# One transformer layer on one core: the first MLP product in another visiting order, its stores on ScalarE's queue, its operands in tiles of their own

## The chip, the core and the metric

The kernel runs on one core of a Trainium2 chip. A core has TensorE (matmuls, PE in the profile), VectorE (DVE), ScalarE (ACT), GpSimd (POOL) and SyncE (SP, which only issues transfers); each runs its own instructions in order, and they meet by semaphores. Transfers between the chip's memory (DRAM) and the on-chip memory are issued from an engine's queue and carried by 16 DMA engines. The metric is the device time of one execution in microseconds (us).

## The reference

One layer of a diffusion backbone for 512 latent and 256 context tokens of width 2048, all in float32. Three groups of heads mix the tokens; their outputs are joined and projected; a squared-ReLU MLP of hidden width 8192 follows; both are gated and added to the stream.

```python
sh1, sc1, g1, sh2, sc2, g2 = _ada(c, ada_w[l], ada_b[l])      # silu(c) @ ada_w + ada_b, in six parts
hl = _modulate(_rmsnorm(x, norm1_w[l]), sh1, sc1)
y_c, y_l = _token_mixers(hc, hl, w_in[l], w_out[l], ...)      # y_l = concat(heads) @ w_out
x = x + g1 * y_l
x = x + g2 * _sq_relu_mlp(_modulate(_rmsnorm(x, norm2_w[l]), sh2, sc2), mlp_w1[l], mlp_w2[l])
return _rmsnorm(x, final_norm_w)

def _sq_relu_mlp(h, w1, w2):
    a = jax.nn.relu(jnp.einsum('btd,df->btf', h, w1))
    return jnp.einsum('btf,fd->btd', a * a, w2)
```

## The kernel before

**Precision.** Every large product is made of three: an operand is split into a rounded part and the rest (`hi`, `lo`), and `mm3` issues hi x hi, lo x hi and hi x lo as three matmuls (L171, L172, L173) into the same bank. A weight is loaded as float32 (`raw`, 128 x 1024, 0.5 MB), cast to `whi` by ScalarE (L94) and subtracted into `wlo` by VectorE (L95).

**Stages.** To 1048 us: normalisation, input projection, token mixers. Then the *output product* (four column groups of eight weight units, bank `yp`); beside it the rest of the adaLN product runs on VectorE (L120, loads at L133), its `raw` tiles from the same ring of three as the weights'. Then the *MLP input*: 64 transposes by matmul, four for each of 16 column groups (L956, `pt<-dg,x`), modulation by ScalarE (L972), and the sums and splits of the operands `hh`, `hl`, `hbh`, `hbl`. Then the two MLP products.

**Seven products for eight.** Both MLP products work by halves of both operands in the manner of Strassen and Winograd: seven products N1 to N7 of sums of halves stand for eight. `combine` (L938 to L941) makes the sums of the activations; the sums of the weights are made on the fly: N5 adds b12 to the N1 tile (VectorE, L1020), N6 and N4 add b22 and b21 to it by a transfer that accumulates (issued by POOL, L1024 and L1032), N7 adds N3's tile to b12's (POOL, L1029).

**The first product** has 32 blocks q of 256 hidden columns. A *visit* is one N of one block: 8 x 3 matmuls of 256 columns. Results meet in three banks per block: X takes N1, N6, N7 and N4, one on top of the other; Y takes N5 and N3; Z takes N2. Between two visits to X an engine must read the sum so far: after N1 ScalarE copies it (L1066), after N6 VectorE subtracts it from a copy of Y (L1073), after N7 the same (L1075), after N4 ScalarE copies it (L1077). Only then may the next visit add to the bank. Then ReLU and square (L1080, L1081), `combine`, a split into `xh` and `xl` (L1085, L1086), and two stores of 0.9 MB into `acd` (L1088, SyncE's queue).

**The order around the change.** The Python list `visits(32)` is TensorE's order. A tile scheduler places the other engines' instructions by data and by priority (`pri`): weights run ahead as far as the rings of tiles allow (seven `raw`, five pairs of splits), and each queue is then followed in order. So SyncE issues loads (L1009) and `acd` stores (L1088) in one sequence, and a store whose data isn't there holds up the loads behind it.

**The second product** has 16 blocks of seven visits of 24 matmuls of 512 columns; it loads its activations back from `acd` (`ao`, 1 MB, L1144) and adds each bank to `y`. At the end the gate (L1110), the residual `xr` (loaded at L1196, added by POOL, L1106), squares (L1117), the multiply by the norm's weight (POOL, L1119) and the row scaling follow.

Of the kernel before, what the change touches and what calls it, by code (L numbers as in the profile page):

```python
# [17 lines left out]
P = 128  # L18
# [29 lines left out]
def trunk_kernel(ctx: ExitStack, tc: tile.TileContext, a: dict, out: bass.AP, dbg: dict):  # L48
# [60 lines left out]
    def ada_units(blocks, fin):  # L109
# [12 lines left out]

        done = None
        for blk in blocks:
            with pri(APRI):
                ac = adap.tile([P, 512], F32, tag="adac", name="adac", bufs=2)
                G.memset(ac, 0.0)
                G.dma_start(out=ac[0:1, :], in_=a["ada2b"][blk:blk + 1, :])
            for u in range(8):
                add()  # L130
                with pri(APRI):
                    raw = wp.tile([P, 1024], F32, tag="raw", name="raw", bufs=3)
# [69 lines left out]
    hh = hp.tile([P, NK, T], F32R, name="hh")  # L202
    hl = hp.tile([P, NK, T], F32R, name="hl")
# [672 lines left out]
    ada = ada_units(range(12, 16), row_store)  # L876
    for n in range(4):
# [3 lines left out]
        for u in range(8):  # L881
            hi, lo = wunit(a["wo"][n, u], 1024)
# [42 lines left out]

    ctxm = ExitStack()
# [4 lines left out]
    hah = hh.rearrange("p k t -> p (k t)").rearrange("p (o k t) -> p o k t", o=4, k=8)  # L931
    hal = hl.rearrange("p k t -> p (k t)").rearrange("p (o k t) -> p o k t", o=4, k=8)

    PLACE = {"N1": 4, "N2": 5, "N3": 1, "N4": 6, "N5": 0, "N6": 2, "N7": 3}

    def combine(x):
# [4 lines left out]
        V.scalar_tensor_tensor(x[:, 1], x[:, 2], -1.0, x[:, 5], op0=ALU.mult, op1=ALU.subtract)  # L941

    hc = ctxc.enter_context(tc.tile_pool(name="hc", bufs=1))
    dg = [hc.tile([P, P], F32, name=f"dg{m}") for m in range(4)]
# [5 lines left out]
    for m in range(4):  # L950
        nc.sync.dma_start(out=x2d[m], in_=x2[:, m])
# [6 lines left out]
    order = [k for p in range(8) for k in (p, p + 8)]  # L958
    for k in order[:2]:
        pts[k] = acc.tile([P, 4, P], F32, tag="acc", name="pt")  # L960
        flip(k, (0, 1, 2))
    for i, k in enumerate(order):
        if i < 2:
# [4 lines left out]
        pt = pts[k].rearrange("p (h m) t -> p h (m t)", h=2)  # L968
        p = k % 8
        if k < 8:  # L970
            hx = hc.tile([P, 8, 256], F32, tag="hx", name="hx", bufs=3)
        S.activation(hx[:, 4:8:3] if k < 8 else hx[:, 5:7], pt, AF.Identity, bias=mod[:, 0, k:k + 1], scale=mod[:, 1, k:k + 1])  # L972
        if k >= 8:
            combine(hx)
            S.copy(hbh[:, :, p], hx[:, 4:7])
            V.tensor_sub(hbl[:, :, p], hx[:, 4:7], hbh[:, :, p].bitcast(F32))  # L976
            S.copy(hah[:, :, p], hx[:, 0:4])
            V.tensor_sub(hal[:, :, p], hx[:, 0:4], hah[:, :, p].bitcast(F32))  # L978
    ctxc.close()
    ctxp.close()  # L980

    def h_op(o, k):
        return (hah[:, o, k], hal[:, o, k]) if o < 4 else (hbh[:, o - 4, k], hbl[:, o - 4, k])

    class Weights:


        def __init__(self, extra, n_raw, n_split, start=None):
            self.extra, self.n_raw, self.n_split = extra, n_raw, n_split
            self.raws = self.splits = 0  # L990

        def raw(self):
            i = self.raws % (3 + self.n_raw)
            self.raws += 1
            if i < 3:
                return wp.tile([P, 1024], F32, tag="raw", name="raw", bufs=3)
            return self.extra.tile([P, 1024], F32, tag="raw2", name="raw", bufs=self.n_raw)

        def split(self, raw):
            i = self.splits % (2 + self.n_split)  # L1000
            self.splits += 1
            if i < 2:
                return split(wp, raw, 1024, 2)
            into = [self.extra.tile([P, 1024], F32R, tag=t + "2", name=t, bufs=self.n_split) for t in ("whi", "wlo")]
            return split(None, raw, 1024, 2, into)

        def load(self, src):
            t = self.raw()
            nc.sync.dma_start(out=t, in_=src)  # L1009
            return t  # L1010

        def operand(self, name, src, held, by):

            b11, b12, b21, b22 = src
            with pri(WPRI):
                if name in ("N1", "N2", "N3"):
                    t = held[name] = self.load({"N1": b11, "N2": b21, "N3": b22}[name])
                elif name == "N5":
                    t, held["b12"] = held["N1"], self.load(b12)
                    V.tensor_add(t, t, held["b12"])  # L1020
                elif name == "N6":
# [3 lines left out]
                    else:  # L1025
                        by.tensor_add(t, t, held["N3"])
# [16 lines left out]


    ctx1 = ExitStack()
    p1 = ctx1.enter_context(tc.tile_pool(name="p1", bufs=1, side="right"))
    wts = Weights(p1, 4, 3)
    held, bank, made, ac = {}, {}, {}, {}
    for q, name in visits(32):
# [6 lines left out]
        if new:  # L1056
            bank[q, which] = acc.tile([P, 512], F32, tag="acc", name="pa")
        b_ = bank[q, which][:, :256]
        for k in range(8):
            xh, xl = h_op(PLACE[name], k)  # L1060
            mm3(b_, wh[:, k], wl[:, k], xh, xl, new and k == 0, k == 7, skip=True)
        with pri(EPRI):
            if name in ("N1", "N5", "N3"):
                r = made[q, name] = p1.tile([P, 256], F32, tag="r", name="r", bufs=3)
# [13 lines left out]
        if name == "N4":  # L1078
# [8 lines left out]
            for i, y in enumerate((xh, xl)):  # L1087
                nc.sync.dma_start(out=acd[q // 4].rearrange("o p i b t -> p o i b t")[:, :, i, q % 4], in_=y.bitcast(F32))  # L1088
# [5 lines left out]
    p2 = ctx.enter_context(tc.tile_pool(name="p2", bufs=1, reuse_waits="tile"))  # L1094
    pr = ctx.enter_context(tc.tile_pool(name="pr", bufs=1, side="right", reuse_waits="tile"))
    wts = Weights(p2, 12, 3)
# [3 lines left out]
    def gate(m, n, last=None):  # L1100
# [12 lines left out]
    def squares(m, n, end=False):  # L1113
# [4 lines left out]
        if not end:  # L1118
            G.tensor_mul(y[:, m, cs], y[:, m, cs], fw[:, cs])  # L1119

    def finish_row(m, n):
# [5 lines left out]
        for c in rest:  # L1127
            c_ = slice(c * 512, (c + 1) * 512)
            if c == rest[-1]:
# [8 lines left out]
    for b, name in visits(nb):  # L1138
# [7 lines left out]
        w = [wts.operand(name, [a["w2"][g, j, h, i] for i in range(4)], held[b][h], V) for h in range(2)]  # L1146
        if b == 0 and name == "N1":
            y = p2.tile([P, 4, D], F32, name="y")
            gb2 = p2.tile([P, D], F32, name="gb2")
# [40 lines left out]
        if last:  # L1190
            if name == "N1":
                xr = {}
# [133 lines left out]
```

## Time and profile before

| | us |
|---|---|
| median of 3 runs (2672.55 to 2679.81) | 2678.2 |
| the profiled execution | 2679.46 |
| its span, first to last instruction | 2677.7 |
| TensorE busy | 2511.1 (94%) |
| VectorE busy | 1841.2 (69%) |
| ScalarE busy | 1156.0 (43%) |
| GpSimd busy | 435.5 (16%) |
| output product, MLP input, first and second MLP product begin at | 1048, 1242, 1270, 2010 |

The busy share is a mean over stages with different limits, so the stages are read apart: a table by stretch, then the waits of the engine that bounds it. In a row of a timeline the number in brackets is the idle time just before the instruction, and behind the arrow is what ended it. In a row of waits stand the engine and line that waited, what released it, and the total, the number and the longest of the waits. The clock is that granted to TensorE, as a share of full speed.

### The profile page before, as it was taken

The numbers are of one execution on the slowest core, as the hardware profiler recorded it, in microseconds if no ns is written. First come the engines' busy times: TensorE is split into PE (matmuls) and PEld (weight loads), VectorE is DVE, ScalarE is ACT, GpSimd is POOL, SyncE is SP. The second block draws the span as 40 slices with busy tenths as digits, with TensorE's granted clock in tenths as the row PEclk, the third lists the DMA queues.
The fourth block names the chain that finished last, engine by engine and source line by source line (L and its number), as shares of the span: only waits on it lengthen the run. The fifth ranks groups of instructions, "written<-read, shape, count | busy, mean of one in ns | idle before, by whom it ended". The sixth has DMA issues, their size and how long they took to land. (4 is left out here: it accounts for less than half of the span.)

```text
span 2677.7 us, 38869 instructions
## 1 busy us (share of the span) xinstructions
PE 2511.1 (94%) x15418; PEld 2274.0 (85%) x15418; DVE 1841.2 (69%) x2390; ACT 1156.0 (43%) x1595; POOL 435.5 (16%) x387
## 2 busy tenths in 40 slices
PE   8999999999999999998898989999887999999995
PEld 6879999998999988777898989999885888888874
DVE  8885666755444556555766767676666788988896
ACT  7664445522222234224555545555444433333333
POOL 0030000001001010001212222222212111111135
PEclk9999999999999999999899999999998999999998
DMA  9843333335454564655677878787769787777753
GB/s 327 296 165 111 109 117 111 128 109 175 131 166 144 158 185 149 222 191 178 185 222 216 232 214 226 214 235 215 209 199 343 243 249 249 219 238 229 230 169 119
DMA packets 182277, 524.03 MB, mean 196 GB/s; under 512 B 18864, under 2 KB 76464, under 8 KB 173264
## 3 DMA queue, kind: packets, MB, share of 16 engines
q1 hardware_dynamic: 157008, 444.78, 49.4%
q0 software_dynamic: 25088, 76.77, 13.8%
q8 instruction: 121, 1.98, 0.3%
q14 instruction: 60, 0.49, 0.1%
HBM read 446.47 MB, written 74.97 MB: 195 GB/s over the span
## 5 line engine op out<-in xcount | busy, mean ns | idle before, releaser
L94 ACT CAST whi<-raw 128x1024 fp32r<-128x1024 f32 (+1 forms) x644 | 661.1, 1038 | 942.1 <-PE yp L173 432.8
L95 DVE TENSOR_TENSOR wlo<-raw,whi 128x1024 fp32r<-128x1024 f32 (+1 forms) x644 | 863.1, 1347 | 282.9 <-ACT whi L94 281.6
L171 PE MATMUL yp<-whi,ao 128*128 128x512 f32 x896 | 350.8, 392 | 37.3 <-DVE gt L1110 18.7
L120 DVE SCALAR_TENSOR_TENSOR adac<-raw,csil,adac 128x512 f32<-128x512 f32 x256 | 192.0, 750 | 260.4 <-DMA raw<-in_ada_dram 251.5
L172 PE MATMUL yp<-wlo,ao 128*128 128x512 f32 x896 | 350.7, 391 | 4.6 <-DVE wlo L95 4.6
L171 PE MATMUL pa<-hh,whi 128*128 128x256 f32 x1024 | 300.3, 293 | 58.3 <-DVE ac L1073 52.3
L173 PE MATMUL yp<-whi,ao 128*128 128x512 f32 x896 | 349.9, 391 | 0.0
L172 PE MATMUL pa<-hl,whi 128*128 128x256 f32 x1024 | 297.5, 291 | 2.4 <-DVE hl L978 2.4
L173 PE MATMUL pa<-hh,wlo 128*128 128x256 f32 x1024 | 297.2, 290 | 0.0
L171 PEld LDWEIGHTS pa<-hh,whi 128*128 128x128 f32 x1024 | 204.1, 199 | 64.3 <-ACT r L1066 32.5
L171 PEld LDWEIGHTS yp<-whi,ao 128*128 128x128 f32 x896 | 169.0, 189 | 74.5 <-DVE gt L1110 19.1
L1029 POOL TENSOR_TENSOR raw<-raw 128x1024 f32<-128x1024 f32 x64 | 173.3, 2708 | 312.2 <-DMA raw<-in_w_dram 136.2
L171 PE MATMUL pa<-hbh,whi 128*128 128x256 f32 x768 | 218.8, 285 | 3.0 <-ACT hx L972 1.6
L172 PE MATMUL pa<-hbl,whi 128*128 128x256 f32 x768 | 218.7, 285 | 1.5 <-DVE hbl L976 1.5
L173 PE MATMUL pa<-hbh,wlo 128*128 128x256 f32 x768 | 218.6, 285 | 0.5 <-DVE wlo L95 0.5
L172 PEld LDWEIGHTS pa<-hl,whi 128*128 128x128 f32 x1024 | 204.0, 199 | 3.4 <-DVE hl L978 3.4
L173 PEld LDWEIGHTS pa<-hh,wlo 128*128 128x128 f32 x1024 | 203.6, 199 | 0.5
L172 PEld LDWEIGHTS yp<-wlo,ao 128*128 128x128 f32 x896 | 169.2, 189 | 41.0 <-DVE wlo L95 5.9
L173 PEld LDWEIGHTS yp<-whi,ao 128*128 128x128 f32 x896 | 169.3, 189 | 35.2
L171 PEld LDWEIGHTS pa<-hbh,whi 128*128 128x128 f32 x768 | 148.4, 193 | 3.9 <-ACT hx L972 1.8
L172 PEld LDWEIGHTS pa<-hbl,whi 128*128 128x128 f32 x768 | 148.6, 193 | 1.9 <-DVE hbl L976 1.9
L173 PEld LDWEIGHTS pa<-hbh,wlo 128*128 128x128 f32 x768 | 148.5, 193 | 0.7 <-DVE wlo L95 0.7
(382 smaller groups left out, 5253.6 us busy)
## 6 DMA issues: line engine op xcount, KB each, us to landing
raw<-in_w_dram SPq DMA_DIRECT2D x256, 512.0 KB, 6.0
raw<-in_ada_dram SPq DMA_DIRECT2D x192, 512.0 KB, 4.2
ao<-acd SPq DMA_DIRECT2D x56, 1024.0 KB, 7.4
raw<-in_w_dram POOLq DMA_DIRECT2D x96, 512.0 KB, 7.5
acd<-xh SPq DMA_DIRECT2D x32, 896.0 KB, 7.8
acd<-xl SPq DMA_DIRECT2D x32, 896.0 KB, 8.6
raw<-in_nb_dram SPq DMA_DIRECT2D x48, 512.0 KB, 3.6
raw<-in_wo_dram SPq DMA_DIRECT2D x32, 512.0 KB, 3.9
```

The lines of the kernel that those rows point to most:

```text
L94: S.copy(hi[:, :n], raw)
L95: V.tensor_sub(lo[:, :n], raw, hi[:, :n].bitcast(F32))
L120: V.scalar_tensor_tensor(ac, raw[:, kk * 512:(kk + 1) * 512], csil[:, 2 * u + kk:2 * u + kk + 1], ac, op0=ALU.mult, op1=ALU.add)
L171: TE.matmul(o, lh, rh, start=start, stop=False, skip_group_check=skip)
L172: TE.matmul(o, lh, rl, start=False, stop=False, skip_group_check=skip)
L173: TE.matmul(o, ll, rh, start=False, stop=stop, skip_group_check=skip)
L1029: G.tensor_add(t, t, held["N3"])
```

## The change

- **Output product.** The adaLN loads get a ring of three tiles of their own; of every four weight units two use further split tiles.
- **Operands.** `hh` and `hl` become four tiles each, and the three operands of `hbh`, `hbl` a pair of tiles each (`hb00` to `hb21`), so that a matmul waits for its own operand.
- **MLP input.** All 16 column groups are transposed and modulated in order; then the sums and the splits are made operand by operand, in halves, N1's first. The subtraction that POOL made in `combine` is VectorE's. The stores `x2d` are on ScalarE's queue.
- **First product.** `visits1` replaces `visits`. Z's bank comes from another pool. N1's loads have a ring of three, all others one of six; pairs of splits are four. N7's weight sum is VectorE's. The `acd` stores are on ScalarE's queue.
- **Second product.** Pools whose tiles are waited for one by one; `y` and `gb2` are made ahead; N7's weight sum stays on POOL, N6's on VectorE. In the last block `xr` is loaded at N5 into six weight tiles and one `ao` tile; POOL multiplies by the norm's weight for two of the four row groups only, VectorE does the others' in one instruction.

```diff
-    hbh = hb.tile([P, 3, 8, 256], F32R, name="hbh")
-    hbl = hb.tile([P, 3, 8, 256], F32R, name="hbl")
+    H += [[hb.tile([P, 8, 256], F32R, name=f"hb{o}{i}") for i in range(2)] for o in range(3)]
...
-        G.tensor_sub(x[:, 3], x[:, 4], x[:, 7])
+        V.tensor_sub(x[:, 3], x[:, 4], x[:, 7])
...
-        nc.sync.dma_start(out=x2d[m], in_=x2[:, m])
+        S.dma_start(out=x2d[m], in_=x2[:, m])
...
+    def h_split(o, x, q):
+        S.copy(H[o][0][:, q], x[:, q])
+        V.tensor_sub(H[o][1][:, q], x[:, q], H[o][0][:, q].bitcast(F32))
...
+        if k % 4 == 3:
+            q = qs_[k % 8 // 4]
+            if k < 8:
+                h_split(4, a11, q)
+                V.tensor_sub(a11[:, q], a11[:, q], a21[:, q])
+            else:
+                h_split(5, a12, q)
+                V.tensor_sub(a21[:, q], a22[:, q], a21[:, q])
...
                     t = held["b12"]
-                    G.tensor_add(t, t, held["N3"])
+                    (by or V).tensor_add(t, t, held["N3"])
...
+    def visits1(n):
+        out_ = [(0, "N1"), (0, "N2"), (1, "N1"), (1, "N2"), (0, "N5"), (1, "N5"), (0, "N3"), (0, "N6"), (1, "N3"),
+                (0, "N7"), (1, "N6"), (0, "N4")]
+        for b in range(2, n):
+            out_ += [(b, "N1"), (b, "N5"), (b - 1, "N7"), (b, "N2"), (b, "N3"), (b, "N6"), (b - 1, "N4")]
+        return out_ + [(n - 1, "N7"), (n - 1, "N4")]
...
-    wts = Weights(p1, 4, 3)
+    raw2, split2 = fresh(p1w, "raw2", 4), pair(p1w, "whi2", "wlo2", 2)
+    wts = Weights(lambda name: int(name != "N1"), [[wp_raw], [early] * 2 + [raw2] * 4],
+                  [wp_split] * 2 + [split2] * 2)
...
-                nc.sync.dma_start(out=acd[q // 4].rearrange("o p i b t -> p o i b t")[:, :, i, q % 4], in_=y.bitcast(F32))
+                S.dma_start(out=acd[q // 4].rearrange("o p i b t -> p o i b t")[:, :, i, q % 4], in_=y.bitcast(F32))
...
-            G.tensor_add(o, o, xr[m][:, cs])
+            G.tensor_add(o, o, xr[m, n // 2][:, 512 * (n % 2):512 * (n % 2 + 1)])
...
-        if not end:
+        if not end and m > 1:
             G.tensor_mul(y[:, m, cs], y[:, m, cs], fw[:, cs])
...
-                for m in {"N1": (0,), "N5": (1,), "N2": (2,), "N3": (3,)}.get(name, ()):
-                    xr[m] = pr.tile([P, D], F32, tag="ao", name="xr", bufs=8)
-                    nc.sync.dma_start(out=xr[m], in_=x2d[m])
+                elif name == "N5":
+                    for m in range(1, 4):
+                        for c in range(2):
+                            t = xr[m, c] = wts.raw(name)
+                            nc.sync.dma_start(out=t, in_=x2d[m][:, c * 1024:(c + 1) * 1024])
```

TensorE, in the middle of the first product, before: the first matmul of each of five visits. The number behind `pa` is the bank; `pa_13509` is block b's bank X, and the visits are N6(b), N1(b+1), N7(b), N5(b+1), N4(b).

```order
L171 MATMUL pa_13509<-hh_130,whi_13708 128x256
...
L171 MATMUL pa_13743<-hbh_11025,whi_13739 128x256
...
L171 MATMUL pa_13509<-hh_130,whi_13771 128x256
...
L171 MATMUL pa_13807<-hh_130,whi_13803 128x256
...
L171 MATMUL pa_13509<-hbh_11025,whi_13835 128x256
```

Now, from N6(b) on: bank X of block b is `pa_13719`, and the visits are N6(b), N4(b-1), N1(b+1), N5(b+1), N7(b).

```order
L171 MATMUL pa_13719<-hh2_132,whi_13876 128x256
...
L171 MATMUL pa_13485<-hb20_11035,whi_13906 128x256
...
L171 MATMUL pa_13953<-hb00_11031,whi_13949 128x256
...
L171 MATMUL pa_13987<-hh0_130,whi_13983 128x256
...
L171 MATMUL pa_13719<-hh3_133,whi_14015 128x256
```

The second visit to the same bank stood two visits after N6's and now stands four after it: one visit of another bank lay between, now three do.

ScalarE, one block of the first product from the relu on, before (`x2`, `x3`: so many in a row):

```order
L1068 ACTIVATE r<-pa 128x256
L94 CAST whi<-raw 128x1024
L1077 COPY ac<-pa 128x256
L1080 ACTIVATE ac<-ac 128x1024
L1081 ACTIVATE ac<-ac 128x1024
L94 CAST whi<-raw 128x1024
L1085 CAST xh<-ac 128x1792
L1068 ACTIVATE r<-pa 128x256
L94 CAST whi<-raw 128x1024 x2
```

And now, with the copy of bank X after N4 (L1133) and the two stores of the block:

```order
L1133 COPY ac<-pa 128x256
L1136 ACTIVATE ac<-ac 128x1024
L1137 ACTIVATE ac<-ac 128x1024
L1122 COPY r<-pa 128x256
L94 CAST whi<-raw 128x1024
L1141 CAST xh<-ac 128x1792
L1124 ACTIVATE r<-pa 128x256
L94 CAST whi<-raw 128x1024
L1144 DMA acd_106<-xh 128x7x256
L94 CAST whi<-raw 128x1024
L1144 DMA acd_106<-xl 128x7x256
L94 CAST whi<-raw 128x1024
```

Two store issues now stand among the casts of weights: that of `xh` behind its own cast and one of weights, that of `xl` one more cast of weights later.

SyncE, at the passage from the first to the second product, before (L1009 weight loads, L1088 `acd` stores, L1144 loads of the second product's operands):

```order
L1009 DMA raw<-in_w_dram 128x1024 x3
L1088 DMA acd_112<-xh 128x7x256
L1088 DMA acd_112<-xl 128x7x256
L1144 DMA ao<-acd_105 128x2048 x7
L1144 DMA ao<-acd_106 128x2048
L1088 DMA acd_112<-xh 128x7x256
L1088 DMA acd_112<-xl 128x7x256
L1009 DMA raw<-in_w_dram 128x1024 x18
```

And now (L1047 weight loads, L1209 operand loads):

```order
L1047 DMA raw<-in_w_dram 128x1024 x131
L1209 DMA ao<-acd_105 128x2048 x2
L1047 DMA raw<-in_w_dram 128x1024
L1209 DMA ao<-acd_105 128x2048
L1047 DMA raw<-in_w_dram 128x1024 x2
L1209 DMA ao<-acd_105 128x2048
L1047 DMA raw<-in_w_dram 128x1024 x2
L1209 DMA ao<-acd_105 128x2048
L1047 DMA raw<-in_w_dram 128x1024 x2
```

The last four stores and the operand loads stood ahead of the second product's weight loads; now no store is in this queue, and operand and weight loads alternate.

## Rows read from the trace of the kernel before

**Rows 1.** Busy time of each engine by stretch of the span.
```profile
core 0: us, PE busy (x) PEld busy (x) DVE busy (x) ACT busy (x) POOL busy (x), PEclk, DMA share, GB/s
1048.00:1242.00 194.00, 182.59 (x776) 146.95 (x775) 111.89 (x148) 57.42 (x85) 11.66 (x20) 0.98 0.61 203
1242.00:1270.00 28.00, 19.14 (x134) 17.92 (x134) 21.43 (x43) 19.78 (x33) 5.53 (x8) 0.88 0.51 174
1270.00:1303.00 33.00, 25.98 (x163) 23.33 (x162) 26.39 (x29) 19.38 (x25) 11.94 (x7) 0.79 0.42 129
1303.00:2009.00 706.00, 649.01 (x5215) 642.52 (x5214) 488.29 (x466) 367.08 (x433) 168.24 (x122) 0.97 0.77 219
2009.00:2050.00 41.00, 22.00 (x83) 16.85 (x84) 19.36 (x15) 13.30 (x16) 7.23 (x3) 0.75 1.02 404
2050.00:2606.00 556.00, 556.00 (x2454) 460.40 (x2453) 483.35 (x462) 223.36 (x218) 108.12 (x64) 1.00 0.74 230
2606.00:2678.00 72.00, 37.96 (x153) 29.67 (x151) 49.64 (x72) 26.81 (x57) 37.33 (x26) 0.81 0.35 117
```

**Rows 2.** Waits of TensorE in the first product, 1303 to 2009 us.
```profile
PE pa L171 <- DVE ac L1073: 52.3, 21, 5.9
```

**Rows 3.** Timeline of TensorE at one of these waits: start, us, instruction.
```profile
1406.61 0.28 PE L173 MATMUL pa<-hbh,wlo 128*128 128x256 f32 x1
...
1410.43 0.36 PE L171 MATMUL pa<-hh,whi 128*128 128x256 f32 x1 [3.54 <-DVE ac L1073]
```

**Rows 4.** Timeline of VectorE: output product, then the first product.
```profile
1173.34 0.75 DVE L120 SCALAR_TENSOR_TENSOR adac<-raw,csil,adac 128x512 f32<-128x512 f32 x1 [5.82 <-DMA raw<-in_ada_dram]
...
1406.79 2.02 DVE L1086 TENSOR_TENSOR xl<-ac,xh 128x1792 fp32r<-128x1792 f32 x1 [0.67 <-ACT xh L1085]
...
1409.87 0.41 DVE L1073 TENSOR_TENSOR ac<-r,pa 128x256 f32<-128x256 f32 x1
...
1449.60 3.18 DVE L95 TENSOR_TENSOR wlo<-raw,whi 128x1024 fp32r<-128x1024 f32 x1 [0.45 <-ACT whi L94]
```

**Rows 5.** Waits of TensorE in the output product, 1048 to 1242 us.
```profile
PE yp L172 <- DVE wlo L95: 10.3, 4, 3.6
```

**Rows 6.** Waits of TensorE between the products, 2009 to 2050 us.
```profile
PE yp L171 <- ACT whi L94: 17.2, 2, 15.6
```

**Rows 7.** Timeline of SyncE: one store's issue, and the second product's loads.
```profile
1406.79 0.38 SPq L1088 DMA_DIRECT2D acd<-xh  x1
...
2020.80 26.58 SPq L1009 DMA_DIRECT2D raw<-in_w_dram  x15
```

**Rows 8.** Waits of TensorE at the end, 2606 to 2680 us.
```profile
PE yp L171 <- DVE gt L1110: 18.7, 1, 18.7
PE yp L172 <- DVE wlo L95: 4.0, 2, 2.6
```

**Rows 9.** Groups by line, 1303 to 2009 us: count, busy, mean ns, idle before.
```profile
L95 DVE TENSOR_TENSOR wlo<-raw,whi 128x1024 fp32r<-128x1024 f32 x217 | 292.4, 1362 | 119.4 <-ACT whi L94 118.8
L1020 DVE TENSOR_TENSOR raw<-raw 128x1024 f32<-128x1024 f32 x31 | 38.0, 1225 | 9.8 <-DMA raw<-in_w_dram 9.0
L938 DVE TENSOR_TENSOR ac<-ac 128x256 f32<-128x256 f32 x31 | 30.1, 970 | 2.4 <-ACT ac L1081 2.3
```

**Rows 10.** Waits of SyncE in the first product, 1303 to 2009 us.
```profile
SPq L1088 <- ACT r L1068: 145.9, 31, 17.1
SPq L1088 <- DVE xl L1086: 57.8, 31, 3.9
```

**Rows 11.** Timeline of TensorE at the first product's first matmul.
```profile
1269.63 0.39 PE L171 MATMUL pa<-hbh,whi 128*128 128x256 f32 x1 [1.61 <-ACT hx L972]
```

**Rows 12.** Timeline of SyncE and of POOL at the end.
```profile
2623.54 5.76 SPq L1196 DMA_DIRECT2D xr<-x2d  x2
2628.62 8.84 POOL L1106 TENSOR_TENSOR y<-y,xr 128x512 f32<-128x512 f32 x5 [0.87 <-DMA xr<-x2d]
```

**Rows 13.** DMA issues of the first product: count, KB each, us to landing.
```profile
raw<-in_w_dram SPq DMA_DIRECT2D x120, 512.0 KB, 7.8
```

More of the change, by code (lines that the diff above doesn't have):

```diff
@@ L107, in trunk_kernel, with ada_units @@
     mod = adap.tile([P, 2, NK], F32, name="mod")
-    def ada_units(blocks, fin):
+    def ada_units(blocks, fin, ring=None):
         late = []
@@ L201, in trunk_kernel, with __init__, __getitem__ @@
     hp = ctxh_.enter_context(tc.tile_pool(name="hT", bufs=1, side="right"))
-    hh = hp.tile([P, NK, T], F32R, name="hh")
-    hl = hp.tile([P, NK, T], F32R, name="hl")
+    class Four:
+        def __init__(self, name):
+            self.tiles = [hp.tile([P, 4, T], F32R, name=f"{name}{i}") for i in range(4)]
+        def __getitem__(self, at):
+            return self.tiles[at[1] // 4][(at[0], at[1] % 4) + at[2:]]
+    hh, hl = Four("hh"), Four("hl")
     ams = hp.tile([P, NK, 4], F32, name="ams")
@@ L881, in trunk_kernel @@
         for u in range(8):
-            hi, lo = wunit(a["wo"][n, u], 1024)
+            into = None
+            if n_unit % 4 > 1:
+                into = [postb.tile([P, 1024], F32R, tag=t, name=t, bufs=2) for t in ("whi3", "wlo3")]
+            n_unit += 1
+            hi, lo = wunit(a["wo"][n, u], 1024, into=into)
             step(ada)
@@ L917, in row_rstd, with fresh, pair, new @@
         return y
+    def fresh(pool, tag, bufs):
+        first = [pool.tile([P, 1024], F32, tag=tag, name="raw", bufs=bufs)]
+        return lambda: first.pop() if first else pool.tile([P, 1024], F32, tag=tag, name="raw", bufs=bufs)
+    def pair(pool, hi, lo, bufs):
+        def new():
+            return [pool.tile([P, 1024], F32R, tag=t, name=n, bufs=bufs) for t, n in ((hi, "whi"), (lo, "wlo"))]
+        first = [new()]
+        return lambda: first.pop() if first else new()
     ctxm = ExitStack()
@@ L950, in trunk_kernel @@
     for m in range(4):
-        nc.sync.dma_start(out=x2d[m], in_=x2[:, m])
+        S.dma_start(out=x2d[m], in_=x2[:, m])
+    Av = [hc.tile([P, 2, 8, 256], F32, name=f"A{i}") for i in range(2)]
+    a11, a21, a12, a22 = Av[0][:, 0], Av[0][:, 1], Av[1][:, 0], Av[1][:, 1]
     pts = {}
@@ L956, in flip @@
             TE.matmul(pts[k][:, m], x2[:, m, k * P:(k + 1) * P], dg[m], start=True, stop=True)
-    order = [k for p in range(8) for k in (p, p + 8)]
-    for k in order[:2]:
+    def h_split(o, x, q):
+        S.copy(H[o][0][:, q], x[:, q])
+        V.tensor_sub(H[o][1][:, q], x[:, q], H[o][0][:, q].bitcast(F32))
+    for k in range(6):
         pts[k] = acc.tile([P, 4, P], F32, tag="acc", name="pt")
         flip(k, (0, 1, 2))
-    for i, k in enumerate(order):
-        if i < 2:
+    qs_ = (slice(0, 4), slice(4, 8))
+    for k in range(NK):
+        if k < 6:
             flip(k, (3,))
@@ L979, in trunk_kernel, with __init__, next, raw @@
+    for o, x in ((1, a12), (2, a21), (3, a11), (6, a22)):
+        for q in qs_:
+            h_split(o, x, q)
     ctxc.close()
     ctxp.close()
-    def h_op(o, k):
-        return (hah[:, o, k], hal[:, o, k]) if o < 4 else (hbh[:, o - 4, k], hbl[:, o - 4, k])
     class Weights:
[L988 to L997, printed above, removed]
-        def split(self, raw):
[L1000 to L1008, printed above, removed]
+        def __init__(self, ring_of, raws, splits):
+            self.ring_of, self.raws, self.splits = ring_of, raws, splits
+            self.used = {}
+        def next(self, ring, tiles):
+            i = self.used.get(ring, 0)
+            self.used[ring] = i + 1
+            return tiles[i % len(tiles)]()
+        def raw(self, name):
+            ring = self.ring_of(name)
+            return self.next(ring, self.raws[ring])
+        def split(self, raw):
+            return split(None, raw, 1024, 2, self.next("split", self.splits))
+        def load(self, name, src):
+            t = self.raw(name)
@@ L1145, in trunk_kernel @@
         t = aops[g, name]
[L1146 to L1149, printed above, removed]
+        w = [wts.operand(name, [a["w2"][g, j, h, i] for i in range(4)], held[b][h], G) for h in range(2)]
         new = name in ("N1", "N5", "N2")
```

78 lines of the change are left out of this document (47 added, 31 removed).

## The prediction

> **What bounds the kernel now.** I read the table by stage first [rows 1]: for each stretch its length, the busy time of each engine, the granted clock and the DMA share. The second MLP product (2050 to 2606 us) is TensorE without a gap: 556.00 us busy in 556.00, clock 1.00. The first MLP product (1303 to 2009) is not: 649.01 busy in 706.00, clock 0.97. So the time to be had lies in the first product and in the short stretches between stages, and the next view is what TensorE waits for in each.
>
> In the first product 52.3 us of the 57.0 idle go to one place: 21 waits of up to 5.9 us for the subtraction at L1073 [rows 2]. That subtraction takes the sum after visit N6 out of bank X before N7 may add to it. Between N6 and N7 of a block the old order has one other visit, N1 of the next block, 24 matmuls or 2.9 us at the 0.12 us that a matmul of 256 columns takes (706 us less idle and clock loss, below, over 5215). The timeline shows why 2.9 us don't do [rows 3, 4]: N1's last matmul starts at 1406.61; VectorE is then in L1086 (2.02 us from 1406.79), behind it a weight split, and L1073 starts only at 1409.87 and takes 0.41; TensorE goes on at 1410.43 after 3.54 us of waiting.
>
> The other stretches, in the same two views. Output product (1048 to 1242): 10.3 us in four waits for a weight split L95, clock 0.98 [rows 1, 5]; at one of them VectorE had stood 5.82 us for an adaLN weight load [rows 4], whose tiles come from the same ring of three as the product's own weights. MLP input (1242 to 1303): 61.00 us with 45.12 busy and clocks of 0.88 and 0.79. Between the products (2009 to 2050): 22.00 busy in 41.00, of which 17.2 are two waits for whi [rows 6]; SyncE issues the fifteen weight loads only from 2020.80 [rows 7], behind the last acd stores. The end (2606 to 2678): 37.96 busy in 72.00, with one wait of 18.7 us for gt at L1110 [rows 8].
>
> **The change part by part.** The sum is made against the profiled execution, 2679.46 us with a span of 2677.7; the median of the runs shown is 2678.2, 1.3 lower.
>
> *First product.* Loss now: 57.0 idle, and the clock: 0.03 of 706, some 21 (the mean is rounded: 18 to 25). The stretch without waits shows 1.00 and every stretch with waits less [rows 1], so I let the clock loss go with the waits. Together 78, 2.5 a block over 31 blocks. The new order puts three visits between N6 and N7 in bank X (N4, N1, N5: 8.6 us) and three between N7 and N4 (N2, N3, N6). L1073 needs 0.41 and what is queued ahead of it on VectorE, at most one L1086 and two L95: 0.4 + 2.0 + 2 x 1.4 = 5.2 [rows 4, 9]. So the wait goes. What is late next is VectorE's own load: 488.29 us in 31 blocks, 15.8 a block, plus the two additions that POOL did (L1029, L939), which at VectorE's price for such shapes (L1020 and L938, 1225 and 970 ns, [rows 9]) are 2.2: 18.0 of the 20.2 us that 168 matmuls take. Part of the 15.8 is lengthened: one L95 beside POOL's L1029 took 3.18 [rows 4], the mean is 1362 ns [rows 9]; without POOL's additions I expect 16. So it fits in the mean, with 2 to 4 us a block to spare, and I leave 8 us for places where it doesn't. Gain 70; bounds 40 (one us a block is lost) and 78 (nothing is).
>
> *The acd stores move to ScalarE's queue.* SyncE stood 145.9 us for xh and 57.8 for xl in this stage [rows 10], 6.6 a block, with weight loads queued behind. Now these waits stand in ScalarE's queue: xh's is the cast just ahead on that engine, and xl's costs at most what lies between its cast and VectorE's split. Behind the store are casts of weights, four pairs of split tiles deep. An issue takes 0.38 us on SyncE [rows 7]; ScalarE's own is not shown for this tile, so I take the same: 0.8 a block beside ScalarE's 367.08 / 31 = 11.8 [rows 1], and count nothing, hidden by 7.6 us of slack. If that cover is gone it is the slower rival below.
>
> The Trainium skill (DMA: Bandwidth & Descriptors, "Issuing engines are not separate DMA queues") speaks against this step: DMAs issued from the several engines share the same 16 DMA engines and interleave, and issuing from more of them saves only the sequencer's issue time. By that rule the move is worth 62 x 0.38, or 24 us of SyncE's time and none of TensorE's; the row on SyncE shows waits in order, 203.7 us, which the rule does not count. My sum gives the move no term of its own, so both readings give the same time.
>
> *Output product.* The adaLN loads get a ring of their own, two of four weight units other split tiles. Of 10.3 us of waits and some 4 of clock (0.02 of 194) I take 9; from 0 (VectorE still works in order through the adaLN sums) to 15.
>
> *MLP input.* The first product's first matmul now stands at 1269.63, behind a wait of 1.61 us for a scaling [rows 11]. Work per operand in halves lets N1 begin when its operand is there, while N3, N6 and N4 are split later; but all 16 scalings come before in order, three POOL subtractions become VectorE's, and b12's load waits for memory of the flips' tiles. VectorE is busy 47.82 of 61.00 us here [rows 1] and gets more. I take a gain of 4, a quarter of TensorE's 15.9 us of idle; from a loss of 13 (VectorE becomes the bound, and the 13 us in which it doesn't work come on top) to a gain of 10, two thirds of that idle.
>
> *Between the products.* SyncE's loads of the second product no longer stand behind the acd stores, and their tiles come free one by one. Of 19 us idle I take 11 back. What is late next is the DMA: the share is 1.02 at 404 GB/s already [rows 1], and the 15 loads of 0.5 MB with the operands of 1 MB need 19 us at that rate, of which some 8 come before the first pairs stand. From 0 to 20.
>
> *The end.* SyncE issued two of the four xr loads at 2623.54 [rows 12], and POOL's additions that need them ran 2628.62 on for 8.84 us; squares, and so gt, came after, and the wait of 18.7 followed. xr is now loaded at N5 of the last block, and fewer products lie on POOL. What is late next is the split of the last N4 weights, which waits for an accumulating load and stands ahead of the gate's product on VectorE. The stage loses 22.7 to waits [rows 8] and some 3 to the clock while busy; I keep 8 and 3 of these, so the gain is 15; from 0 to 25.
>
> Sum: -70 - 9 - 4 - 11 - 15 = -109, so 2679.5 - 109 = 2570, and with the 1.3 to the median 2569. I say 2570.
>
> **Rivals.** *VectorE is the bound* in the first product: with 18.0 of 20.2 in order, subtractions come late in the new place and 1.3 us a block are lost, 40 more: 2610. For it: L95 has the most busy time there [rows 9]. Against it: three visits of cover.
>
> *The DMA engines are.* The share was 0.77 over 706 us [rows 1]; the same bytes in 628 + 8 make 0.85. If loads (7.8 us from issue to landing now, [rows 13]) stretch, a block takes 21.5: also 2610. Against it: 0.74 in the second product at no loss.
>
> *The first product gains, the edges don't* (transition and end turn one wait into another): 2570 + 26 = 2596.
>
> *Slower: ScalarE stands before its stores.* If the 6.6 us a block of SyncE's waits all come to stand on ScalarE, the casts behind are 6.6 late each block; one visit (2.9) of finished pairs covers part, or none: 3.7 to 6.6 a block lost, 115 to 205 us, in the mean 160: 2570 + 160 = 2730. It decides from 3.5 us a block (109 / 31). Against it: most of the 145.9 is SyncE waiting for ScalarE's own earlier work, which in ScalarE's queue is no wait.
>
> *The change doesn't do what it says*: the pools let tiles free later than written, so that the loads come as late as before and the stall is only renamed: 2660 to 2690, about the same.
>
> **How the numbers follow.** What a measurement can tell from no change is about 0.3%, 8 us. Forecast (2545 to 2595) 0.46; VectorE 0.18; DMA 0.14; edges 0.10; slower by ScalarE 0.06; nothing done 0.06. Of the last I give half to no change, a third to slower. Faster is 0.46 + 0.18 + 0.14 + 0.10 = 0.88 and a little, 0.89; same 0.03; slower 0.08. The range reaches from 2535, where the edges give all and the first product all, to 2630, past the two cases at 2610 with their own spread; it leaves out the slower case, the undone one, and a few in a hundred below.
>
> **What would show it.** In the profile after: TensorE's waits in the first product without L1073's successor (the subtraction after N6), busy share above 0.97, clock 1.00; SyncE's waits for xh and xl gone and none of more than 2 us in ScalarE at its stores; no wait for gt over 8 us at the end; the first weight loads of the second product landing before its first matmul is due. I am wrong if TensorE waits 1 us a block or more for a split, or if ScalarE's idle time at the stores is 3 us a block.

## The result, and the profile after

| | us |
|---|---|
| changed, median of 4 runs (2600.21 to 2605.4) | 2602.68 |
| before, median of 4 runs beside them (2672.55 to 2679.81) | 2677.57 |
| ratio, 95% interval | 0.9723 [0.9706, 0.974] |
| profiled execution, its span | 2605.4, 2603.6 |

The forecast was 2570 with a range from 2535 to 2630. The time fell by 75 us where 109 were summed. The kernel after by stage, as in [rows 1] (columns: stretch, its length, busy us of PE, PEld, DVE, ACT, POOL with counts, clock, DMA share, GB/s):

```profile
1050.00:1244.00 194.00, 178.84 (x770) 145.22 (x769) 116.76 (x152) 55.58 (x85) 11.50 (x20) 0.96 0.61 210
1244.00:1264.00 20.00, 16.56 (x131) 15.88 (x130) 8.60 (x21) 13.38 (x25) 0.55 (x1) 0.91 0.71 262
1264.00:1300.00 36.00, 20.35 (x148) 19.24 (x146) 35.23 (x32) 23.02 (x28) 2.63 (x3) 0.84 0.58 161
1300.00:1935.00 635.00, 631.78 (x5227) 631.42 (x5228) 466.76 (x526) 373.24 (x434) 51.82 (x61) 0.99 0.85 238
1935.00:2000.00 65.00, 55.55 (x223) 43.06 (x222) 43.66 (x39) 31.01 (x36) 12.97 (x6) 0.92 0.91 325
2000.00:2040.00 40.00, 40.00 (x174) 32.41 (x173) 31.73 (x29) 18.03 (x20) 8.29 (x4) 1.00 1.02 370
2040.00:2540.00 500.00, 500.00 (x2163) 404.80 (x2162) 430.21 (x416) 189.55 (x181) 96.88 (x59) 1.00 0.74 225
2540.00:2604.00 64.00, 34.73 (x138) 26.21 (x136) 48.99 (x71) 21.57 (x51) 27.47 (x18) 0.83 0.27 82
```

The first product is full: 631.78 of 635 busy, where 57 were idle. The start of that product, the output product and the end have idle time and a low clock as before. The next table takes each stage's length from the start times of its matmuls. Where the row doesn't say "whole", the matmuls themselves are taken off, at the pace of the stretches without a gap: 0.12007 us for 256 columns (first product, after) and 0.22667 us for 512 (second product, before). The columns "before" and "after" are then what is left, the time lost:

| us lost | before | after | gain | forecast |
|---|---|---|---|---|
| output product, first to last matmul's start (whole) | 193.9 | 195.3 | -1.4 | 9 |
| from there to N1's first matmul (whole) | 27.8 | 20.5 | 7.3 | 4, with the next row |
| first product, matmuls 0 to 168 | 13.8 | 21.0 | -7.2 | |
| first product, 168 to 5200 | 70.5 | 0.0 | 70.5 | 70 |
| its last visits and the second product's first 336 matmuls | 31.8 | 21.2 | 10.6 | 11 |
| second product, 336 to 2500 | 0.0 | 10.1 | -10.1 | 0 |
| rest to the last instruction | 37.4 | 33.1 | 4.3 | 15 |
| sum | | | 74.0 | 109 |

What TensorE waits for after the change, in four stretches (line that waited, releaser, total, times, longest): the output product, the start of the first product, the passage, the end.

```profile
PE yp L171 <- ACT whi L94: 13.1, 1, 13.1
...
PE pa L171 <- ACT r L1122: 10.3, 1, 10.3
...
PE yp L171 <- ACT whi L94: 4.9, 1, 4.9
...
PE yp L171 <- DVE gt L1173: 12.7, 2, 12.0
PE yp L172 <- DVE wlo L95: 2.1, 3, 0.8
```

The 52.3 us of [rows 2] and the 17.2 of [rows 6] are gone or small, the 18.7 of [rows 8] is 12.0, and two waits are new. The places behind them, in the timelines after (start, us, engine, instruction, idle before and its releaser):

```profile
1071.62 1.99 ACT L94 CAST whi<-raw 128x1024 fp32r<-128x1024 f32 x2 [0.80 <-DVE hl L787]
...
1297.54 0.37 ACT L1122 COPY r<-pa 128x256 f32<-128x256 f32 x1 [4.97 <-DVE hl L991]
...
1950.79 1.69 ACT L1141 CAST xh<-ac 128x1792 fp32r<-128x1792 f32 x1 [7.18 <-DMA acd<-xh]
...
2560.57 0.63 ACT L1180 ACTIVATE sq<-y 128x512 f32<-128x512 f32 x1 [10.09 <-POOL y L1169]
...
2572.80 2.13 DVE L95 TENSOR_TENSOR wlo<-raw,whi 128x1024 fp32r<-128x1024 f32 x1 [2.54 <-ACT whi L94]
2574.85 0.68 DVE L1173 TENSOR_TENSOR gt<-yp,gb 128x512 f32<-128x512 f32 x1
```

In the output product the cast into the further split tiles starts only when the token mixers' last split (L787) is done: the new pool lies on memory of their tiles, and adaLN loads wait there too. At the start of the first product the copy of N1's bank (L1122) starts only when VectorE has made the last operand splits (L991): the built program puts the copy's tile at 92704, inside the MLP input's tile A0 (92128 to 108512), and so it must wait until A0 has been read. At the passage ScalarE's cast of xh waits 7.18 us for the store of the block before, and the next weight cast stands behind it. At the end the gate's product stands on VectorE behind the split of N4's last weights, whose cast stood on ScalarE behind squares that waited for POOL.

The loss from 336 to 2500 is of another kind: no wait, clock 1.00, and still 2163 matmuls in 500 us where the kernel before made 2207:

```profile
2050.00:2550.00 500.00, 500.00 (x2207) 414.04 (x2206) 429.86 (x411) 202.25 (x198) 91.28 (x55) 1.00 0.77 237
```

By their start times, in the mean of each tile, the matmuls that stream from the two old pairs of split tiles are followed by the next in 227 to 232 ns, those from the three new pairs in 233.2 to 233.4; before, all in 226.7. The built program puts the new pairs at 131040 and on, 96 modulo 128 bytes; before they lay at 75552 and on, 32 modulo 128, as do the old pairs in both kernels.

### The profile page after: what moved, and what is told of

Its sections match the earlier page's. It is cut to its first block, busy times and chain, and to the rows that moved or that the text cites. A ratio compares the mean times of both kernels' runs of the same rounds, so it can differ in the third digit from the quotient of the medians.

```text
span 2603.6 us, 38694 instructions
## 1 busy us (share of the span) xinstructions
PE 2499.1 (96%) x15418; PEld 2257.0 (87%) x15418; DVE 1821.4 (70%) x2440; ACT 1156.6 (44%) x1589; POOL 298.4 (11%) x309
## 4 chain that ended last, share of the span: by engine, by line
PE 44%; DVE 4%; DMA 2%; ACT 1%; issue 1%; POOL 0%; ACTq 0%; SPq 0%; DVEq 0%; POOLq 0%
PE pa L172 8%; PE pa L171 8%; PE pa L173 8%; PE yp L172 7%; PE yp L171 7%; PE yp L173 7%; DVE wlo L95 2%; DMA acd<-xl 2%; DMA raw<-in_w_dram 1%; DVE y L1168 0%; DVE y L1248 0%; ACT whi L94 0%; DVE hl L991 0%; ACT A L1003 0%; PE pt L986 0%
## 5 line engine op out<-in xcount | busy, mean ns | idle before, releaser
L95 DVE TENSOR_TENSOR wlo<-raw,whi 128x1024 fp32r<-128x1024 f32 (+1 forms) x644 | 826.2, 1289 | 248.4 <-ACT whi L94 247.6
L171 PE MATMUL pa<-hh,whi 128*128 128x256 f32 x1024 | 292.2, 285 | 13.6 <-ACT r L1122 10.3
L172 PE MATMUL pa<-hl,whi 128*128 128x256 f32 x1024 | 291.9, 285 | 0.1
L173 PE MATMUL pa<-hh,wlo 128*128 128x256 f32 x1024 | 291.7, 285 | 0.0
L172 PE MATMUL pa<-hb,whi 128*128 128x256 f32 x768 | 218.2, 284 | 3.8 <-DVE hb L991 3.8
L171 PE MATMUL pa<-hb,whi 128*128 128x256 f32 x768 | 217.8, 284 | 1.3 <-DVE ac L1131 1.3
L173 PE MATMUL pa<-hb,wlo 128*128 128x256 f32 x768 | 218.1, 284 | 0.0
L172 PEld LDWEIGHTS pa<-hb,whi 128*128 128x128 f32 x768 | 148.0, 193 | 4.2 <-DVE hb L991 4.2
L171 PEld LDWEIGHTS pa<-hb,whi 128*128 128x128 f32 x768 | 147.8, 192 | 1.5 <-issue 1.5
L173 PEld LDWEIGHTS pa<-hb,wlo 128*128 128x128 f32 x768 | 148.1, 193 | 0.0
L1248 DVE TENSOR_TENSOR y<-y,yp 128x512 f32<-128x512 f32 x202 | 137.0, 678 | 4.3 <-PE yp L173 1.1
```

The costliest lines, as they stand in the source:

```text
L95: V.tensor_sub(lo[:, :n], raw, hi[:, :n].bitcast(F32))
L171: TE.matmul(o, lh, rh, start=start, stop=False, skip_group_check=skip)
L172: TE.matmul(o, lh, rl, start=False, stop=False, skip_group_check=skip)
L173: TE.matmul(o, ll, rh, start=False, stop=stop, skip_group_check=skip)
L1248: (V.tensor_add if sign > 0 else V.tensor_sub)(o, o, src)
```

## Experiments

The first product is read in one stretch that all kernels share, 1330 to 1900 us, by the count of TensorE's matmuls in it; 570 / 0.12 is 4750. Ratios are to the kernel before, timed on the same chip.

**The old order in the changed kernel.**
```diff
-    for q, name in visits1(32):
+    for q, name in visits(32):
```


> The changed kernel with the first product's visits in the old order; all else stays changed. Theory A (the order pays: three visits instead of one between N6 and N7 hide the subtraction): the 21 or so waits for it come back, 52 us and the clock that goes with them, so 2655 to 2690 us. Theory B (what pays is the rest of the stage's edits: stores off SyncE's queue, N7's sum off POOL, rings by operand): TensorE stays without waits, 2600 to 2620 us.

Measured 2611.07, ratio 0.9746 [0.9725, 0.9767]; the interval overlaps that of the changed kernel. Theory A fell: the stage is as full as with the new order, and what the profiled execution loses against the changed kernel it loses outside this stretch.
```profile
1330.00:1900.00 570.00, 570.00 (x4753) 570.00 (x4752) 431.14 (x479) 340.82 (x396) 48.30 (x57) 1.00 0.88 248
```
Its timeline of VectorE shows why one visit of cover is enough there:
```profile
1511.56 0.42 DVE L1129 TENSOR_TENSOR ac<-r,pa 128x256 f32<-128x256 f32 x1
1512.44 1.22 DVE L95 TENSOR_TENSOR wlo<-raw,whi 128x1024 fp32r<-128x1024 f32 x1 [0.47 <-ACT whi L94]
1514.03 2.03 DVE L1142 TENSOR_TENSOR xl<-ac,xh 128x1792 fp32r<-128x1792 f32 x1 [0.37 <-ACT xh L1141]
```
The subtraction after N6 (L1129) stands ahead of the xl split; in [rows 4] it stood behind it.

What else is new in the stage shows in ScalarE's casts of weights, 1340 to 1900 us, before and then after (behind the second bar: idle time before them, and what ended it). In the kernel before the casts waited 136.9 us for loads, now 27.6:
```profile
L94 ACT CAST whi<-raw 128x1024 fp32r<-128x1024 f32 x173 | 177.2, 1045 | 215.7 <-DMA raw<-in_w_dram 136.9 <-PE pa L172 68.1 <-PE pa L173 6.9
...
L94 ACT CAST whi<-raw 128x1024 fp32r<-128x1024 f32 x195 | 201.3, 1049 | 156.8 <-PE pa L172 101.2 <-DMA raw<-in_w_dram 27.6 <-ACT whi L94 13.0
```

**The new order alone in the kernel before** (`visits1` in place of `visits`, nothing else).


> The kernel before with nothing changed but the order of the first product's visits. Theory A: most of the 78 us that the stage lost comes back, 2600 to 2620 us. Theory B: the loads still stand behind the stores in SyncE's queue and one ring serves all operands, so the wait is only renamed: 2650 to 2690 us.

Measured 2660.74, ratio 0.9925 [0.991, 0.994]: Theory A fell, and the order alone is worth a quarter. From matmul 168 to 5200 it loses 44.7 us in place of 70.5. No wait for that subtraction is left, but TensorE waits 22.7 us for copies of bank Y: N3 may add to N5's result only when ScalarE has copied it (L1077 in that kernel). ScalarE's casts still wait 125.8 us for loads (136.9 in the same stretch of the kernel before).
```profile
PE pa L171 <- ACT r L1077: 22.7, 9, 3.6
...
1330.00:1900.00 570.00, 547.04 (x4459) 544.20 (x4458) 402.01 (x395) 310.18 (x371) 132.90 (x105) 0.98 0.81 232
...
L94 ACT CAST whi<-raw 128x1024 fp32r<-128x1024 f32 x180 | 183.4, 1047 | 245.2 <-DMA raw<-in_w_dram 125.8 <-DVE raw L1020 105.3 <-issue 8.4
```

**The acd stores back in SyncE's queue.**
```diff
-                S.dma_start(out=acd[q // 4]...
+                nc.sync.dma_start(out=acd[q // 4]...
```


> The changed kernel with the acd stores back in SyncE's queue. By my sum, which gave the move no term: 2595 to 2612 us, the same as changed, with SyncE waiting some 6 us a block for xh and xl. Theory B: the loads stand behind the stores, TensorE waits for weights, 2630 us or more.

Measured 2625.98, ratio 0.9796 [0.9781, 0.981]: between the two ranges, some 20 us slower than changed, and none of it in the stage (4752 matmuls in the 570 us). It is lost at the passage: from the first product's last visits to the second's first 336 matmuls 43.0 us against 21.2.
```profile
1966.97 1.33 SPq L1047 DMA_DIRECT2D raw<-in_w_dram  x3
1968.35 0.43 SPq L1144 DMA_DIRECT2D acd<-xh  x1
...
1980.29 1.68 ACT L1141 CAST xh<-ac 128x1792 fp32r<-128x1792 f32 x1 [12.65 <-DMA acd<-xh]
...
1986.87 0.79 PE L171 MATMUL yp<-whi,ao 128*128 128x512 f32 x1 [20.36 <-ACT y L1240]
```
The store stood in SyncE's queue behind the second product's loads; the next block's xh must wait for it to land, since there is one tile; and ScalarE, in order, held the bank copies that TensorE needed.

**N7's weight sum back on POOL** in the first product (`G.tensor_add`).


> The changed kernel with N7's weight sum of the first product back on POOL. If VectorE has room to spare there, as I reckoned (2 to 4 us a block), nothing moves: 2597 to 2608 us; L95 gets longer again (mean above 1.3 us). If the sum on VectorE was needed because POOL's additions lengthen VectorE's splits: 2620 us or more.

Measured 2607.53, ratio 0.9723 [0.9706, 0.9739]: the same, 4752 matmuls. L95's mean stayed at 1221 ns, against the expectation. That doesn't show that POOL's sums leave the splits alone: by their start times and durations, no split in the stretch ran beside one of them. In the kernel "rings and the new order" below, 27 of 194 do, and these take 2.40 us in place of 1.22:
```profile
1499.46 2.40 POOL L1067 TENSOR_TENSOR raw<-raw 128x1024 f32<-128x1024 f32 x1 [3.71 <-DVE raw L1058]
...
1500.54 2.40 DVE L95 TENSOR_TENSOR wlo<-raw,whi 128x1024 fp32r<-128x1024 f32 x1 [1.17 <-ACT whi L94]
```
In the kernel before, 25 of 172 ran beside POOL's additions and took 2.38 us in the mean, the others 1.22. With the loads in time and the new order it costs nothing: that stage is full.

**One ring of nine tiles.**
```diff
-    wts = Weights(lambda name: int(name != "N1"), [[wp_raw], [early] * 2 + [raw2] * 4],
+    wts = Weights(lambda name: 0, [[wp_raw] * 3 + [early] * 2 + [raw2] * 4],
```


> The changed kernel, its nine weight tiles of the first product as one ring in turn instead of three for N1 and six for the rest. Theory C (the loads pay: in one ring a load in SyncE's queue waits for N1's tile, which lives through N5, N6 and N4, and holds up all loads behind it, so splits and then subtractions come late): ScalarE waits 100 us or more for loads again, 2630 to 2660 us. Theory D (two more tiles pay, not the grouping): 2600 to 2612 us, as changed.

Measured 2629.98, ratio 0.9813 [0.9797, 0.983]: outside Theory D's range and at the edge of Theory C's. ScalarE waits 49.3 us for loads, half of what Theory C expected, and 29 us are lost from matmul 168 to 5200.
```profile
1330.00:1900.00 570.00, 554.00 (x4520) 552.17 (x4520) 408.32 (x461) 324.19 (x378) 46.52 (x55) 0.98 0.84 237
```

**Seven tiles in two rings** (`raw2` with two tiles in place of four).


> The changed kernel with seven weight tiles in the first product as before, three for N1 and four for the rest. Theory C: hardly anything is lost, 2600 to 2620 us. Theory D: the stage loses as before, 2630 us or more.

Measured 2651.94, ratio 0.9895 [0.9878, 0.9913], against Theory C; ScalarE waits 90.8 us for loads, and 33 us are lost from matmul 168 to 5200.
```profile
1330.00:1900.00 570.00, 549.47 (x4495) 544.67 (x4494) 398.87 (x453) 320.09 (x375) 45.05 (x53) 0.99 0.83 234
```

**Two rings of the same seven tiles in the kernel before** (N1 takes the ring of three, the rest the ring of four).


> The kernel before with nothing changed but that N1's loads of the first product take the ring of three tiles and all others the ring of four. Theory C: ScalarE's 137 us of waits for loads and most of the 78 us of loss go, 2600 to 2625 us. Theory D, or the old theory A (order) with nothing but order to help: 2665 to 2685 us.

Measured 2665.3, ratio 0.995 [0.9932, 0.9968]. ScalarE still waits 103.3 us for loads. From matmul 168 to 5200 it loses 41.6 us in place of 70.5, but the first 168 matmuls lose 15 us more than before. Neither C nor D holds alone: the number of tiles and the grouping each pay, and neither suffices.
```profile
1330.00:1900.00 570.00, 540.00 (x4430) 535.39 (x4429) 424.30 (x396) 313.77 (x370) 133.66 (x105) 0.99 0.81 231
```

**Rings only.**
```diff
-        V.tensor_sub(x[:, 3], x[:, 4], x[:, 7])
+        G.tensor_sub(x[:, 3], x[:, 4], x[:, 7])
...
-                    (by or V).tensor_add(t, t, held["N3"])
+                    G.tensor_add(t, t, held["N3"])
...
-    for q, name in visits1(32):
+    for q, name in visits(32):
...
-                S.dma_start(out=acd[q // 4]...
+                nc.sync.dma_start(out=acd[q // 4]...
```


> The changed kernel with four things of the first product undone together: the visits in the old order, the acd stores in SyncE's queue, N7's weight sum and the combine's subtraction on POOL. What stays there are the nine weight tiles in two rings (and the operands in tiles of their own). Theory C (the rings alone pay for the stage): TensorE loses nothing from the stage's second block to its last, and with the 20 us that the stores cost at the passage 2615 to 2645 us. Rival: each of the four is spare alone and one of them is needed: the stage loses 25 us or more again, 2650 us or more.

Measured 2678.23, ratio 0.9993 [0.9983, 1.0002]: Theory C fell, the rival held. The loads are in time (5.8 us of waits for them), and yet 48.0 us are lost from matmul 168 to 5200: 25 waits for the subtraction in the stretch, 1.40 us each. The 22.5 us that this is better than before don't show in the time, since the start of the product, the passage and the second product each lose some 10 us more than in the kernel before.
```profile
L94 ACT CAST whi<-raw 128x1024 fp32r<-128x1024 f32 x181 | 189.1, 1045 | 206.1 <-PE pa L172 113.8 <-issue 83.8 <-DMA raw<-in_w_dram 5.8
...
PE pa L171 <- DVE ac L1129: 34.9, 25, 1.4
...
1330.00:1900.00 570.00, 533.73 (x4403) 529.22 (x4402) 422.24 (x392) 315.02 (x366) 129.84 (x104) 1.00 0.80 231
...
1498.81 2.02 DVE L1142 TENSOR_TENSOR xl<-ac,xh 128x1792 fp32r<-128x1792 f32 x1 [0.66 <-ACT xh L1141]
1500.75 0.41 DVE L1129 TENSOR_TENSOR ac<-r,pa 128x256 f32<-128x256 f32 x1
...
1501.31 0.36 PE L171 MATMUL pa<-hh,whi 128*128 128x256 f32 x1 [1.40 <-DVE ac L1129]
```
Here is the prediction's mechanism by itself: the subtraction right behind the xl split, one visit of cover.

**Rings and the new order** (as before it, with `visits1`).


> The changed kernel with the visits in the new order, and the other three undone: acd stores in SyncE's queue, N7's weight sum and the combine's subtraction on POOL. Against e13_rings_only only the order differs; there TensorE waited 1.40 us in each block for the subtraction after N6, which stood behind the xl split. Theory E (two causes: late loads, which the rings cure, and that subtraction with one visit of cover, which either the order cures or the sums on VectorE, which put it ahead of the xl split): no such wait, no loss from the second block on, 2615 to 2635 us. Rival (the order is worth nothing by itself; only the sums on VectorE cure it): 1.4 us a block remain, 2660 to 2680 us.

Measured 2631.03, ratio 0.9811 [0.9797, 0.9824]. Theory E holds: full, and no wait for the subtraction.
```profile
1330.00:1900.00 570.00, 570.00 (x4752) 570.00 (x4751) 434.43 (x425) 343.43 (x397) 141.83 (x113) 1.00 0.87 248
```

Matmuls in the 570 us, the kernels together, without the two single moves (stores back on SyncE, N7's sum back on POOL: 4752 each). The 7-tile kernels with the sums on POOL are made from the kernel before, which has no operand tiles of their own, five split pairs for four and Z's bank in the same pool as the others:

| | 7 tiles, one ring | 7, two | 9, one | 9, two |
|---|---|---|---|---|
| old order, sums on POOL, stores on SyncE | 4240 (before) | 4430 | | 4403 |
| new order, sums on POOL, stores on SyncE | 4459 | | | 4752 |
| old order, sums on VectorE, stores on ScalarE | | | | 4753 |
| new order, sums on VectorE, stores on ScalarE | | 4495 | 4520 | 4753 (after) |

**64 bytes of padding.**
```diff
+    p2s.tile([P, 16], F32, name="pad")
     split3 = pair(p2s, "whi2", "wlo2", 3)
```


> The changed kernel with 64 bytes of padding ahead of the second product's three new split pairs, so that they start at 32 instead of 96 modulo 128 bytes. In the trace after, a matmul that streams from one of them takes 233.4 ns, from the old pairs mostly 227, in the trace before always 226.7. Theory: the start address modulo 128 costs it; then all return to 226.7 and the time falls by 10 us, 0.4%. Rival: it is the place above 128 KiB in the partition that costs (these pairs moved from 75552 to 131040): then the pitch stays 233 and the time stays.

Measured 2594.12, ratio 0.9676 [0.9661, 0.9691] against 0.9723 [0.9706, 0.974], 0.5% less. In the mean of each tile, the matmuls of the steady stretch are followed by the next in 226.6 to 226.7 ns, from tiles that now start at 131104 and on, still above 128 KiB (131072): the rival fell.
```profile
2035.00:2535.00 500.00, 500.00 (x2208) 414.15 (x2207) 436.97 (x422) 194.93 (x186) 99.20 (x60) 1.00 0.74 228
```

**Four edits on top.**
```diff
-            if n_unit % 4 > 1:
+            if n_unit % 4 > 1 and n > 0:
...
+                elif "sum" in held:
+                    t = held["N1"]
+                    V.tensor_add(t, t, held["N2"])
...
-                if name == "N3":
+                if name == "N1":
+                    r = r1.pop() if r1 else hb.tile([P, 256], F32, tag="rN1", name="r", bufs=1)
+                elif name == "N5":
                     r = adap.tile([P, 512], F32, tag="adac", name="r", bufs=2)[:, :256]
...
+    p2s.tile([P, 16], F32, name="pad")
...
```


> The changed kernel with four edits on top, each read from its own stage of the trace: the 64 bytes of padding (10 us); the output product's further split tiles only from the second column group on (the wait of 13.1 us at 1072.72 and its clock: 10 to 15 us; 0 if VectorE's waits for adaLN loads come back); the copies of N1 and N5 in tiles that do not lie on the MLP input's memory (the wait of 10.3 us at 1297.96: 5 to 13 us, 0 if VectorE's splits are late there anyway); in the last block N4's weights as a sum on VectorE instead of an accumulating load (of the 12 us wait at the end 4 to 8; a loss of 3 if VectorE is late). Together 2560 to 2585 us, a ratio of 0.956 to 0.965 to the kernel before; 0.967 if only the padding pays.

Measured 2578.85, ratio 0.9621 [0.9604, 0.9637]. By stage against the changed kernel: output product 187.4 in place of 195.3 (the wait of 13.1 is gone, one of 6.1 for yt stands in its place); first product's start 12.5 in place of 21.0 (no wait for a copy over 0.3 us is left); the padding 10.1; the end 32.2 in place of 33.1. There the wait for gt fell from 12.0 to 6.5 us, but TensorE waits 4.8 us there for weight splits (2.1 in the changed kernel).

**And the last block's xh and xl in other tiles.**
```diff
+            if q == 31:
+                xh = p1.tile([P, 8, 256], F32R, tag="ac", name="xh", bufs=2)[:, 0:7]
+                xl = x[:, 0:7].bitcast(F32R)
```


> e11_best with one more edit: the last block's xh and xl do not take the tiles of the block before, whose stores are still under way at the passage to the second product; ScalarE waited 7.2 us there for a store and its next weight cast stood behind it. If that is what the 5.5 us wait at the passage is, it goes: 4 to 8 us less than e11_best, ratio 0.959 to 0.961. If the weight loads are late anyway (the DMA engines are at their limit there): 0.962, the same.

Measured 2576.02, ratio 0.9611 [0.9598, 0.9624] against 0.9621 [0.9604, 0.9637]: the intervals overlap, so a gain isn't shown. In the trace the passage costs 17.3 us in place of 21.2; the wait for the cast went, and one of 9.3 for a bank copy came.
```profile
1944.16 0.79 PE L171 MATMUL yp<-whi,ao 128*128 128x512 f32 x1 [9.28 <-ACT y L1254]
```

## Why the prediction was right, and where not

**First product, 70: measured 70.5, for another reason.** The step "the new order puts three visits between N6 and N7, so the wait goes" is true by itself, as the pair of kernels with rings and with or without the new order shows (48 us, 0). But in the changed kernel the order is spare: without it the stage is as full. The prediction read the wait's last releaser, L1073, and took its place behind the xl split for the cause. It didn't ask why VectorE's splits came so late in the kernel before: ScalarE's casts waited for loads, 136.9 us in 1340 to 1900. The changed rings of tiles, which the sum gave no term, brought that to 27.6 (5.8 in the kernel with the rings only); nine tiles in one ring (4520 with the rest of the change) or two rings of seven (4495) don't do it. So there were two causes, and each must be cured: late loads by nine tiles in two rings, the subtraction by the order or by what puts it ahead of the xl split. Lost from matmul 168 to 5200 were 70.5 us with both, 44.7 with the new order alone, 48.0 with the rings and the old order, and nothing with both cured. That 70 came out is in part luck: the sum took the whole loss back for one cure, and the change held both.

Two things stay open. Which of the sums on VectorE and the stores on ScalarE moves the subtraction ahead of the xl split in the old order was not run apart. And all kernels with nine tiles have the operand tiles, Z's bank from another pool and four split pairs too; what these are worth in the stage was not run.

VectorE's load was overstated: 18.0 us a block reckoned, some 15 measured (429 us in the 570). The combine's subtraction (L964), priced at 0.97 us by a row lengthened beside POOL, takes 0.42 there, and the splits take 1.22.

**Stores, no term: 20 us.** The move's own paragraph counted it at nothing, and weighed only the stage; what it saves stands in the passage's 11. With the stores on SyncE the passage costs 21.8 us more. The Trainium skill's rule (DMA: Bandwidth & Descriptors, "Issuing engines are not separate DMA queues"), that issuing from several engines saves only the sequencer's issue time, holds in the stage (4752 and 4753 matmuls) and not at the passage, where a store waited in order behind loads.

**Output product, 9: -1.4.** Most of VectorE's waits for adaLN loads did go (62.3 us to 10.7). This is outside its bounds (0 to 15). The step that failed is that further tiles cost nothing: they lie on memory that the mixers give free late, a wait of 13.1 us.

**Start, 4: 0.1.** N1's first matmul came 7.3 us sooner as said; the 10.3 us wait for a copy whose tile lies on A0 took it back. The bounds held it.

**Passage, 11: 10.6.** The stores had to leave SyncE's queue, as said; that the size held is luck. With the stores left there the passage loses 43.0 us, 11 more than before: there the last stores stand behind loads in that queue, where before the loads stood behind the stores. So the move gained 21.8, and the rest of the change gave half of it back. ScalarE stood 7.2 us at a store's landing there, the slower rival's mechanism, once and not each block. The prediction's 19 us at 404 GB/s is the price of the fifteen weight loads alone, 7.9 MB, and not of the operands with them.

**End, 15: 4.3.** The waiting split ahead of the gate was named; it cost 12.0 us, and with the smaller waits 14.8 stand where 8 were to stay; the clock stayed low (0.83), and behind TensorE's last matmul came 3 us more than before.

**Second product, 0: -10.1.** No step spoke of it; moving tiles changed the start address of the streamed operand.

Of the rivals, VectorE as the bound and the DMA engines as the bound were wrong: 466.76 of 635 busy, and a DMA share of 0.85 with no loss. The edges that don't pay were nearest: 2596 was given for it. Of the prediction's signs those of the first product came true (busy 0.995 of the stretch); those of the edges did not: a wait for gt of 12.0 us, over 8, and one of 4.9 for the second product's first weights.

## What to carry to other kernels

Where an engine waits for a step, look at what that step's queue had been waiting for, back to the loads: a wait's last releaser can be late for a reason two engines away. Where two causes can each hold an engine up, cure each alone before the sum gives the whole loss to one: here the order alone and the rings alone each left more than half of it. Give tiles that live long a ring of their own, and enough tiles to the other. When pools move, compare where new tiles lie, on whose memory and at which start address, as well as when they are asked for.

## What was not expected of the hardware

A float32r matmul of 512 columns whose streamed tile starts at 96 modulo 128 bytes is followed by the next in 233.2 to 233.4 ns, at 32 modulo 128 in 226.7 where all tiles lie so, and 64 bytes of padding bring the one back to the other. Only these two places were compared, in the second product. At 256 columns, in the first product, all streamed tiles lay at 32 modulo 128, and nothing is shown.
